# Token norms taken on columns of tokens, and the recurrent layer's norm moved between the two halves of its first head's contraction

## The chip, the core and the metric

The kernel runs on one core of one Trainium2 chip. The metric is the device time of one execution in microseconds, as a median over runs. The engines named below are PE (TensorE), DVE (VectorE), ACT (ScalarE), POOL (GpSimd) and SP (SyncE, which issues all transfers here); each runs its own instructions in order and they wait for each other through semaphores.

## The reference, cut to what matters

Two residual layers over 2048 tokens of 1024 features, each behind an RMS norm, and a last norm:

```python
def rms_norm(x, w):
    y = x * lax.rsqrt(jnp.mean(x * x, axis=-1, keepdims=True) + RMS_EPS)
    return y * w
...
h = rms_norm(x, norm_w[0]);  x = x + chunked_sgu_mixer(h, ...)   # widths 3 * 2048, then back
h = rms_norm(x, norm_w[1]);  x = x + rglru_mixer(h, ...)         # 12 heads of 128, gate path, scan
return rms_norm(x, norm_f_w)
```

The mean is over the 1024 features of one token, so a norm is one number for each token.

## The kernel before

Features lie on the 128 partitions and tokens along the free axis, so a tile is 128 features by 512 tokens. The tokens are worked in two blocks of 1024 (`i` = 0, 1), each in two halves of 512 (`th`). A product in full precision is made of three matmuls on rounded parts (`mm3`, L286): each operand is split by ACT into a rounded copy (L80) and by DVE into what is left of it (L81).

For each block the program runs: the first norm (`Half.norm`, names `a`), the value projection (`pv`), the gated products (`J`, `Y`, `ps`), the output products (`X`, `Y`, `Z`), the second norm (names `b`), the recurrent layer's heads (`px`, `pg`, then `pr` and `pi` for its gates), its output products (`po`), and the last norm (names `f`). The program's `f` norms of block 0 are written into block 1's value projection, and block 1's `a` norms into block 0's last `po` products.

A norm works like this. `Norm.add` squares each tile on ACT and adds it to an accumulator `sa` of 128 by 512 on DVE. `Norm.finish` multiplies `sa` by a 128 by 128 matrix of ones (`st`, L400), so that all 128 partitions hold the sum of each of the 512 tokens, and takes the root in `rsqrt` on the whole 128 by 512: `nm` on ACT (L374), the square root on ACT (L375), then on DVE a reciprocal (L376) and one step of refinement (L377 to L379). Its result `r` (called `ra`, `rbb`, `rf`) then scales the tiles.

In the recurrent layer the norm is applied behind the projection, since the scale of a token commutes with it: `Head.conv` multiplies the finished `px` by `rb` (L718), convolves (L725, L729), splits the result into `xch` (L734) and `xcl` (L735), and `gates` multiplies these by the gate weights into `pr` and `pi`. The first head (`n` = 0) contracts its 1024 features in two halves `u`, in the order `px` half 0, `pg` half 0, `px` half 1, `pg` half 1; `after(0, 0)` then calls `finish_b`, the two halves of the norm. Head 1's `px` and head 0's `gates` follow.

A scheduler places the instructions of each engine by readiness and priority, so the written order is only a preference. Accumulators of three tiles of two banks (`pj`) and two of one bank (`pb`) are shared by everything on PE; split weights go round in eight buffers (`wops`), and their raw loads in four (`raws`).

Of the kernel before, what the change touches and what calls it, by code (L numbers as in the profile page):

```python
# [9 lines left out]
F32 = mybir.dt.float32  # L10
F32R = mybir.dt.float32r
AF = mybir.ActivationFunctionType
ALU = mybir.AluOpType

P = 128
D = 1024
# [5 lines left out]
TB = 2 * T  # L22
# [29 lines left out]
def trunk(ctx: ExitStack, tc: tile.TileContext, xT, WI, WV, WB, WO, WG, par, wsT, bs, outT):  # L52
    nc = tc.nc

    const = ctx.enter_context(tc.tile_pool(name="const", bufs=1))
# [4 lines left out]
    work = ctx.enter_context(tc.tile_pool(name="work", bufs=12))  # L60
# [3 lines left out]
    def pj(name):  # L64
        return pjp.tile([P, 2, T], F32, tag="pj", name=name)

    def pb(name):
        return pbp.tile([P, T], F32, tag="pb", name=name)

    def wk(name):  # L70
        return work.tile([P, 1032], F32, tag="wk", name=name)[:, :TB].rearrange(
            "p (a t) -> p a t", a=2
        )

    def sm(name, tag="sm"):
        return smp.tile([P, T], F32, tag=tag, name=name)
# [136 lines left out]
    for i in range(NB):  # L213
# [10 lines left out]
        if i == 0:  # L224
            for k in (0, 4):
                n = ahead.pop(0)
# [43 lines left out]
    def take(key):  # L270
        def load(key, make, load):
            if load is not None:
                load()

        def make(key, make, load):
            t = make()
            if key is not None:
                ready[key] = t

        advance(loads, at[key] + FAR, load)  # L280
        advance(makes, at[key] + LOOK, make)
        return ready.pop(key)

    def mm3(out, sh, sl, mh, ml, first, last):
        for n, (s, m) in enumerate(((sh, mh), (sh, ml), (sl, mh))):
            nc.tensor.matmul(  # L286
                out, lhsT=s, rhs=m, start=first and n == 0, stop=last and n == 2,
                skip_group_check=True,
            )
# [5 lines left out]
    def col(c):  # L295
        return pp[:, c : c + 1]

    ones = const.tile([P, P], F32, name="ones")
    eps = const.tile([P, 2], F32, name="eps")
    halo = const.tile([P, NH, 3], F32, name="halo")  # L300
    state = const.tile([P, NH], F32, name="state")
    c8 = const.tile([P, NH], F32, name="c8")
# [4 lines left out]
        nc.tensor.matmul(warm[:, :P], lhsT=ones, rhs=ones, start=True, stop=True)  # L307
    nc.gpsimd.memset(eps[:, 0:1], RMS_EPS)
    nc.gpsimd.memset(eps[:, 1:2], LN_EPS)
    nc.gpsimd.memset(halo, 0.0)  # L310
    nc.gpsimd.memset(state, 0.0)

# [59 lines left out]
    def rsqrt(r, x, m, t, scale, e):  # L372

        nc.scalar.activation(m, x, AF.Identity, bias=eps[:, e : e + 1], scale=scale)  # L374
        nc.scalar.activation(r, m, AF.Sqrt)  # L375
        nc.vector.reciprocal(r, r)  # L376
        nc.vector.tensor_tensor(t, r, r, ALU.mult)  # L377
        nc.vector.scalar_tensor_tensor(t, t, -0.5, m, ALU.mult, ALU.mult)
        nc.vector.scalar_tensor_tensor(r, t, 1.5, r, ALU.add, ALU.mult)  # L379

    class Norm:
# [5 lines left out]
        def add(self, t, eng=nc.vector):  # L387
            for kk in range(2):
# [6 lines left out]
                    eng.tensor_tensor(self.acc, self.acc, q, ALU.add)  # L395
                self.n += 1

        def finish(self, r):
            st = pb(f"st_{self.name}")
            nc.tensor.matmul(st, lhsT=ones, rhs=self.acc, start=True, stop=True)  # L400
            rsqrt(r, st, sm(f"nm_{self.name}"), self.acc, 1.0 / D, 0)

    xv = xT.rearrange("(g k a p) t -> g a p k t", g=2, k=2, a=2, p=P)
    ov = outT.rearrange("(g k a p) t -> g a p k t", g=2, k=2, a=2, p=P)
# [50 lines left out]
    class Pair:  # L455


        def __init__(self, i, m, tp, outs, c21, finish):
            self.i, self.m, self.tp, self.outs = i, m, tp, outs
            self.c21, self.finish = c21, finish  # L460
            self.id = f"{i}_{m}"
# [101 lines left out]
    def y_tile(name):  # L563
        return tc.dram_tile([2, 2, P, 2, T], F32, name=name)
# [139 lines left out]
    class Head:  # L704
# [9 lines left out]
        def conv(self, px, rb):  # L714

            n = self.n
            xb = work.tile([P, 1032], F32, tag="wk", name=f"xb{self.id}")
            nc.vector.tensor_tensor(  # L718
                xb[:, 3 : 3 + TB].rearrange("p (a t) -> p a t", a=2), px, rb, ALU.mult
            )  # L720
            nc.gpsimd.tensor_copy(xb[:, 0:3], halo[:, n, :])
            nc.gpsimd.tensor_copy(halo[:, n, :], xb[:, TB : TB + 3])
            xc = self.xc = wk(f"xc{self.id}")
            xf = self.flat(xc)
            nc.scalar.activation(  # L725
                xf, xb[:, 3 : 3 + TB], AF.Identity, bias=col(C_CB + n), scale=col(C_CW + 4 * n + 3)
            )
            for k in range(3):
                nc.vector.scalar_tensor_tensor(  # L729
                    xf, xb[:, k : k + TB], col(C_CW + 4 * n + k), xf, ALU.mult, ALU.add  # L730
                )
            self.ch = work.tile([P, 2, T], F32R, tag="wk", name=f"xch{self.id}")
            self.cl = work.tile([P, 2, T], F32R, tag="wk", name=f"xcl{self.id}")
            nc.scalar.copy(self.ch, xc)  # L734
            nc.vector.tensor_tensor(self.cl, xc, self.ch.bitcast(F32), ALU.subtract)  # L735
# [44 lines left out]
    def b_branch(i, hb, rb, hooks):  # L780

        yd = [y_tile(f"yb{i}_{r}") for r in range(3)]
        gw = {}
        heads = [Head(i, n, gw, yd) for n in range(NH)]

        def proj(out, n, z, us=(0, 1)):
            for u in us:
                w = take((i, "b", n, z, u))
                for a, th in ((0, 0), (1, 1), (0, 1), (1, 0)):
                    t = hb[a, th, u]  # L790
                    for kk in range(2):
                        o = (2 * kk + a) * P
                        mm3(
                            out[:, th], w[:, 0, o : o + P], w[:, 1, o : o + P], t[:, 0, kk],
                            t[:, 1, kk], u == 0 and a == th and kk == 0,
                            u == 1 and a != th and kk == 1,
                        )

        def after(n, k):
            for f in hooks.get((n, k), ()):  # L800
                f()

        for n in range(NH):
            px = pj(f"px{i}_{n}")
            if n == 0:
                pg = pj(f"pg{i}_{n}")
                for u in range(2):
                    proj(px, n, 0, (u,))
                    proj(pg, n, 1, (u,))
                after(0, 0)  # L810
            else:
                proj(px, n, 0)
                heads[n - 1].gates()
            heads[n].conv(px, rb)
            if n > 0:
                heads[n - 1].decay()
                pg = pj(f"pg{i}_{n}")
                proj(pg, n, 1)
            heads[n].silu(pg, rb)
            if n > 0:  # L820
                heads[n - 1].scan()
            after(n, 1)
        return yd, heads[-1]
# [105 lines left out]
    for i in range(NB):  # L929
# [40 lines left out]
        def ready_b(g, a, th, i=i, x=x, xd=xd, nm=nm, hb=hb):  # L970

            def f():
                t = x[a, th, g]
                nc.sync.dma_start(xd[a, th, g], t)
                o = hb[a, th, g] = top(f"hb{i}_{a}{th}{g}")
                for kk in range(2):
                    w = col(C_NB + 4 * g + 2 * kk + a)
                    nc.scalar.activation(o[:, 0, kk], t[:, kk], AF.Copy, scale=w)
                    nc.vector.scalar_tensor_tensor(
                        o[:, 1, kk], t[:, kk], w, o[:, 0, kk].bitcast(F32), ALU.mult, ALU.subtract  # L980
                    )
                nm[th].add(t)
            return f

        after = {
            (g, p): [ready_b(g, a, th)]
            for g in range(2)
            for p, a, th in ((2, 0, 0), (7, 1, 1), (3, 0, 1), (4, 1, 0))
        }
# [13 lines left out]
        def get_y(r, i=i, y=y):  # L1003
            def f():
                y[r] = load_yb(i, r, yd)
            return f

        yd, tail = b_branch(i, hb, rb, {(0, 0): [finish_b]})
        y[0] = load_yb(i, 0, yd)
        x = {}  # L1010
# [124 lines left out]
```

## Time and profile before

| | |
|---|---|
| median of 3 runs | 2289.09 us (2287.63 to 2290.79) |
| the profiled execution, its own time | 2292.71 us |
| its span in the profile | 2291.0 us |
| PE busy / DVE busy / ACT busy | 97% / 69% / 46% of the span |
| mean granted clock of PE | 0.99 |
| transfers | 327.84 MB, 41% of 16 engines' span |

The span runs from the first to the last instruction that the profile records; the execution's own time is 1.7 us longer, and 3.6 us above the median of the runs. PE's busy share counts matmuls from start to modelled end, so an interval in which PE has waited shows as an entry of the waits, and one in which it was slow as a granted clock below 1.

### The profile page before, as it was taken

To read this page: it belongs to the slowest core of one execution; us is meant where nothing else is said; L and a number is where in the kernel's file an instruction comes from. 1 tells how busy PE (TensorE), PEld (TensorE's weight loads), DVE (VectorE), ACT (ScalarE), POOL (GpSimd) and SP (SyncE) were. 2 spreads that over 40 slices of the span, in tenths; PEclk is the share of its full clock that TensorE was granted. 3 is DMA by queue.
4 is the path that set the end of the run, shared out by engine and by line. 5 is a ranking of instruction groups with operands and counts; after the bars stand their busy time and mean duration, and the time that the engine had idled before them with its cause. 6 is when DMAs were issued, how large, how long until landed. Compare 5 with 4: busy or idle time off the path is not lost.

```text
span 2291.0 us, 25466 instructions
## 1 busy us (share of the span) xinstructions
PE 2213.1 (97%) x9872; PEld 1821.4 (80%) x9872; DVE 1575.7 (69%) x1936; ACT 1057.3 (46%) x1377; POOL 63.2 (3%) x82
## 2 busy tenths in 40 slices
PE   5999999999999899999999999999999989999996
PEld 4787888888788688888788888888878868888884
DVE  6957787676777677775693266676669766776736
ACT  4434444443215677774342144444412347767611
POOL 0000000000000001000000000000000000110000
PEclk9999999999999999999999999999999989999998
DMA  4788353327764122226143233322487512321411
GB/s 148 262 310 307 127 180 111 110 83 270 276 231 141 51 88 88 95 102 231 37 166 110 74 110 111 102 94 100 162 311 256 194 60 69 106 92 65 176 45 74
DMA packets 124040, 327.84 MB, mean 143 GB/s; under 512 B 9616, under 2 KB 26128, under 8 KB 123920
## 3 DMA queue, kind: packets, MB, share of 16 engines
q1 hardware_dynamic: 123920, 326.22, 41.0%
q8 instruction: 77, 1.26, 0.2%
q14 instruction: 43, 0.35, 0.0%
HBM read 232.34 MB, written 93.85 MB: 142 GB/s over the span
## 4 chain that ended last, share of the span: by engine, by line
PE 85%; DVE 8%; DMA 3%; issue 2%; ACT 1%; SPq 0%; DVEq 0%; ACTq 0%
PE J L286 20%; PE pv L286 13%; PE pg L286 11%; PE px L286 10%; PE po L286 10%; PE X L286 6%; PE Y L286 5%; PE Z L286 3%; PE ps L653 2%; PE pr L286 2%; PE pi L286 2%; DMA keep<-wc 1%; DVE ya L81 1%; DMA x<-in_xT 1%; DVE xr L873 0%
## 5 line engine op out<-in xcount | busy, mean ns | idle before, releaser
L286 PE MATMUL pv<-wv,b 128*128 128x512 f32 x1536 | 357.9, 395 | 19.6 <-ACT b L80 15.8
L286 PE MATMUL J<-ha,w 128*128 128x512 f32 x1536 | 368.9, 391 | 0.5 <-DVE u_2b L494 0.5
L286 PEld LDWEIGHTS pv<-wv,b 128*128 128x128 f32 x1536 | 291.4, 190 | 86.4 <-ACT b L80 17.8
L286 PEld LDWEIGHTS J<-ha,w 128*128 128x128 f32 x1536 | 287.6, 188 | 61.5 <-DVE u_2b L494 0.9
L286 PE MATMUL po<-yb,wo 128*128 128x512 f32 x1152 | 265.6, 392 | 2.6 <-DVE xr L862 2.6
L286 PE MATMUL pg<-hb,wb 128*128 128x512 f32 x1152 | 266.6, 390 | 0.0
L286 PE MATMUL px<-hb,wb 128*128 128x512 f32 x1152 | 266.6, 390 | 0.0
L286 PEld LDWEIGHTS po<-yb,wo 128*128 128x128 f32 x1152 | 217.3, 189 | 49.7 <-DVE xr L862 3.0
L286 PEld LDWEIGHTS pg<-hb,wb 128*128 128x128 f32 x1152 | 217.1, 188 | 46.0
L286 PEld LDWEIGHTS px<-hb,wb 128*128 128x128 f32 x1152 | 216.3, 188 | 45.8 <-PE st_b L400 0.5
L286 PE MATMUL J<-b,w 128*128 128x512 f32 x768 | 186.8, 391 | 0.3 <-DVE w L81 0.3
L286 PE MATMUL X<-ya,w 128*128 128x512 f32 x768 | 184.1, 390 | 2.3 <-ACT ya L80 1.3
L286 PEld LDWEIGHTS X<-ya,w 128*128 128x128 f32 x768 | 143.6, 188 | 34.0 <-DVE x L550 2.2
L286 PEld LDWEIGHTS J<-b,w 128*128 128x128 f32 x768 | 142.9, 188 | 30.0 <-DVE w L81 0.7
L80 ACT CAST w<-raw 128x512 fp32r<-128x512 f32 x160 | 99.3, 622 | 139.7 <-issue 66.9
L81 DVE TENSOR_TENSOR w<-raw,w 128x512 fp32r<-128x512 f32 x160 | 109.7, 688 | 61.6 <-ACT w L80 61.2
L80 ACT CAST ya<-ya 128x1024 fp32r<-128x1024 f32 x56 | 57.0, 1049 | 170.7 <-DVE ya L449 92.7
L80 ACT CAST wb<-rb 128x512 fp32r<-128x512 f32 x96 | 58.8, 616 | 99.9 <-PE px L286 49.2
L550 DVE TENSOR_TENSOR x<-x,X 128x1024 f32<-128x1024 f32 x64 | 78.0, 1218 | 35.2 <-PE X L286 35.1
L286 PE MATMUL Z<-ya,w 128*128 128x512 f32 x384 | 94.3, 391 | 3.1 <-DVE ya L81 2.7
L729 DVE SCALAR_TENSOR_TENSOR xc<-xb,pp,xc 128x1024 f32<-128x1024 f32 x72 | 92.3, 1282 | 4.3 <-ACT xc L725 3.5
L286 PE MATMUL Y<-b,w 128*128 128x512 f32 x384 | 93.5, 392 | 0.8 <-DVE sp L657 0.6
(344 smaller groups left out, 2868.0 us busy)
## 6 DMA issues: line engine op xcount, KB each, us to landing
w<-keep SPq DMA_DIRECT2D x112, 512.0 KB, 3.8
raw<-in_w SPq DMA_DIRECT2D x64, 512.0 KB, 3.5
keep<-wc SPq DMA_DIRECT2D x56, 512.0 KB, 5.7
rb<-in_wb SPq DMA_DIRECT2D x48, 512.0 KB, 3.4
rv<-in_v SPq DMA_DIRECT2D x32, 512.0 KB, 4.3
vd<-v SPq DMA_DIRECT2D x32, 512.0 KB, 4.4
vl<-vd SPq DMA_DIRECT2D x32, 512.0 KB, 4.7
ya<-ya SPq DMA_DIRECT2D x16, 1024.0 KB, 5.8
```

The costliest lines, as they stand in the source:

```text
L80: nc.scalar.copy(dst[:, 0], src)
L81: nc.vector.tensor_tensor(dst[:, 1], src, dst[:, 0].bitcast(F32), ALU.subtract)
L286: nc.tensor.matmul(out, lhsT=s, rhs=m, start=first and n == 0, stop=last and n == 2, skip_group_check=True,)
L550: nc.vector.tensor_tensor(t, t, acc[z], ALU.add)
L653: nc.tensor.matmul(pS[:, n * P : (n + 1) * P], lhsT=v[j][th][:, n, cc * P : (cc + 1) * P], rhs=wcv[:, j, :], start=True, stop=True,)
L729: nc.vector.scalar_tensor_tensor(xf, xb[:, k : k + TB], col(C_CW + 4 * n + k), xf, ALU.mult, ALU.add)
```

## The change

The sum over features is now taken with the roles turned: 128 tokens of `sa` are the weights and one column of ones is streamed (`columns`), so `st` holds a token's sum on its own partition, 128 tokens in each of 4 columns. The root is taken by the same six instructions on 128 by 4 elements, in place, in the first columns of `sa`. `row` brings it back onto all partitions: DVE multiplies an identity matrix by each column (128 by 128, four times), PE multiplies ones by that diagonal into `bc`, and ACT copies the 128 by 512 result to `r`. POOL makes the identity once at the start. In the first head of the recurrent layer, `after(0, 0)` is called behind the first half `u` = 0 instead of behind both. Two lines shrink a buffer and a descriptor area to make room for the identity.

```diff
@@ const
+    ident = const.tile([P, P], F32, name="ident")
...
+    nc.gpsimd.affine_select(
+        out=ident, in_=ones, pattern=[[1, P]], compare_op=ALU.is_equal, fill=0.0, base=0,
+        channel_multiplier=-1,
+    )
@@ class Norm
+        def columns(self):
+            st = pb(f"st_{self.name}")
+            for n in range(4):
+                nc.tensor.matmul(
+                    st[:, n : n + 1], lhsT=self.acc[:, n * P : (n + 1) * P], rhs=ones[:, 0:1],
+                    start=True, stop=True,
+                )
+            c = self.c = self.acc[:, 0:12].rearrange("p (k n) -> p k n", k=3)
+            rsqrt(c[:, 0], st[:, 0:4], c[:, 1], c[:, 2], 1.0 / D, 0)
+            return c[:, 0]
+
+        def row(self, r):
+            d = sm(f"nd_{self.name}")
+            b = pb(f"bc_{self.name}")
+            for n in range(4):
+                ns = slice(n * P, (n + 1) * P)
+                nc.vector.tensor_scalar(d[:, ns], ident, self.c[:, 0, n : n + 1], None, ALU.mult)
+                nc.tensor.matmul(b[:, ns], lhsT=ones, rhs=d[:, ns], start=True, stop=True)
+            nc.scalar.copy(r, b)
+
         def finish(self, r):
-            st = pb(f"st_{self.name}")
-            nc.tensor.matmul(st, lhsT=ones, rhs=self.acc, start=True, stop=True)
-            rsqrt(r, st, sm(f"nm_{self.name}"), self.acc, 1.0 / D, 0)
+            self.columns()
+            self.row(r)
@@ b_branch
                 for u in range(2):
                     proj(px, n, 0, (u,))
                     proj(pg, n, 1, (u,))
-                after(0, 0)
+                    if u == 0:
+                        after(0, 0)
@@ wk, conv
-        work.tile([P, 1032], F32, tag="wk", ...)
+        work.tile([P, 1028], F32, tag="wk", ...)
@@ kernel
-    nc = bacc.Bacc("TRN2", target_bir_lowering=False, num_devices=1, dynamic_dma_scratch_size=1024)
+    nc = bacc.Bacc("TRN2", target_bir_lowering=False, num_devices=1, dynamic_dma_scratch_size=512)
```

**PE at the recurrent layer's first head, block 0.** `pg_0`, `px_0` and `px_1` are the accumulators of heads 0 and 1; the suffix `_0` or `_1` of `st_b` and `bc_b` is the half of the tokens. Before:

```order
L286 MATMUL pg_0_5200<-hb_100_5016,wb_01_0_5107 128x512 x6
L286 MATMUL px_0_5199<-hb_001_5096,wb_00_1_5137 128x512 x6
L286 MATMUL px_0_5199<-hb_111_5124,wb_00_1_5137 128x512 x6
L286 MATMUL px_0_5199<-hb_011_5154,wb_00_1_5137 128x512 x6
L286 MATMUL px_0_5199<-hb_101_5184,wb_00_1_5137 128x512 x6
...
L286 MATMUL pg_0_5200<-hb_101_5184,wb_01_1_5167 128x512 x6
L400 MATMUL st_b_0_5313<-sa_b_0_4940,ones 128x512
L400 MATMUL st_b_1_5322<-sa_b_1_4966,ones 128x512
L286 MATMUL px_1_5347<-hb_000_4935,wb_10_0_5201 128x512 x6
```

After the change, at the same place on PE (the line numbers are those of the changed file):

```order
L286 MATMUL pg_0_5228<-hb_100_5044,wb_01_0_5135 128x512 x6
L407 MATMUL st_b_0_5285<-ones,sa_b_0_4968 128x1 x4
L286 MATMUL px_0_5227<-hb_001_5124,wb_00_1_5165 128x512 x6
L286 MATMUL px_0_5227<-hb_111_5152,wb_00_1_5165 128x512 x6
L286 MATMUL px_0_5227<-hb_011_5182,wb_00_1_5165 128x512 x3
L422 MATMUL bc_b_0_5297<-nd_b_0_5296,ones 128x128 x4
L407 MATMUL st_b_1_5307<-ones,sa_b_1_4994 128x1 x4
L286 MATMUL px_0_5227<-hb_011_5182,wb_00_1_5165 128x512 x3
L286 MATMUL px_0_5227<-hb_101_5212,wb_00_1_5165 128x512 x6
L422 MATMUL bc_b_1_5319<-nd_b_1_5318,ones 128x128 x4
L286 MATMUL pg_0_5228<-hb_001_5124,wb_01_1_5195 128x512 x6
```

The sums of the first half of the tokens moved ahead of 48 products (`px_0` and `pg_0`, second half), and the broadcasts stand between them, 15 products behind the first sums and 9 behind the second.

**ACT at the same place.** `wb` is a split weight, `xc` the convolution, `xch` its rounded copy. Before, and then after:

```order
L80 CAST wb_20_0_5377<-rb_20_5228 128x512
L80 CAST wb_20_1_5404<-rb_20_5228 128x512
L80 CAST wb_21_0_5449<-rb_21_5284 128x512
L374 ACTIVATE nm_b_0_5315<-st_b_0_5313,eps 128x512
L375 ACT_TABLE_LOAD
L375 ACTIVATE rbb_5195<-nm_b_0_5315 128x512
L374 ACTIVATE nm_b_1_5324<-st_b_1_5322,eps 128x512
L375 ACTIVATE rbb_5195<-nm_b_1_5324 128x512
```

```order
L80 CAST wb_20_0_5431<-rb_20_5256 128x512
L379 ACTIVATE sa_b_0_4968<-st_b_0_5285,eps 128x4
L380 ACT_TABLE_LOAD
L380 ACTIVATE sa_b_0_4968<-sa_b_0_4968 128x4
L423 COPY rbb_5223<-bc_b_0_5297 128x512
L379 ACTIVATE sa_b_1_4994<-st_b_1_5307,eps 128x4
L380 ACTIVATE sa_b_1_4994<-sa_b_1_4994 128x4
L80 CAST wb_20_1_5458<-rb_20_5256 128x512
L423 COPY rbb_5223<-bc_b_1_5319 128x512
L751 ACTIVATE xc_0_5389<-xb_0_5385,pp 128x1024
L80 CAST wb_21_0_5503<-rb_21_5356 128x512
L760 CAST xch_0_5394<-xc_0_5389 128x1024
```

Two casts of weights that stood ahead of the roots now stand behind the first root, one of them ahead of the second copy.

**DVE at the last norm of block 0, inside block 1's value projection.** `xa`, `xt` and `ha` belong to block 1's gated products, `nd_f` is the diagonal. Before, and then after:

```order
L81 TENSOR_TENSOR b_011_8168<-xt_1_7612,b_011_8168 128x1024
L81 TENSOR_TENSOR b_111_8171<-xt_1_7612,b_111_8171 128x1024
L376 RECIPROCAL rf_0_8186<-rf_0_8186 128x512
L376 RECIPROCAL rf_1_8232<-rf_1_8232 128x512
L377 TENSOR_TENSOR sa_f_0_7857<-rf_0_8186 128x512
L377 TENSOR_TENSOR sa_f_1_7862<-rf_1_8232 128x512
```

```order
L381 RECIPROCAL sa_f_0_7937<-sa_f_0_7937 128x4
L475 TENSOR_TENSOR xa_001_7659<-xt_1_7666,xa_001_7659 128x1024
L382 TENSOR_TENSOR sa_f_0_7937<-sa_f_0_7937 128x4
L81 TENSOR_TENSOR ha_0_5_8433<-xa_000_7655,ha_0_5_8433 128x1024
L383 SCALAR_TENSOR_TENSOR sa_f_0_7937<-sa_f_0_7937 128x4
L475 TENSOR_TENSOR xt_0_7663<-xt_0_7663 128x1024
L384 SCALAR_TENSOR_TENSOR sa_f_0_7937<-sa_f_0_7937 128x4
L475 TENSOR_TENSOR xa_000_7655<-xt_0_7663,xa_000_7655 128x1024
L421 TENSOR_SCALAR nd_f_0_8278<-ident,sa_f_0_7937 128x128 x4
```

Four tiles of 128 by 1024 now stand between the steps of that root, and PE's broadcast of it comes 30 products behind its sums.

## Rows read from the trace of the kernel before

**Rows 1.** The page's chain that ended last, shares of the span by engine.

```profile
PE 85%; DVE 8%; DMA 3%; issue 2%; ACT 1%; SPq 0%; DVEq 0%; ACTq 0%
```

**Rows 2.** Waits of PE: releaser, us in total, times, longest.

```profile
PE pr L286 <- ACT xch L734: 18.4, 2, 9.2
```

**Rows 3.** Timeline, second norm of block 0: start, us, what [idle before <-releaser].

```profile
722.58 0.62 ACT L80 CAST wb<-rb 128x512 fp32r<-128x512 f32 x1 [2.54 <-PE pg L286]
...
733.26 1.88 PE L400 MATMUL st_b<-sa_b,ones 128*128 128x512 f32 x4
...
734.58 11.49 PE L286 MATMUL px<-hb,wb 128*128 128x512 f32 x48
...
735.03 1.28 ACT L375 ACT_TABLE_LOAD   x1
736.32 0.63 ACT L375 ACTIVATE rbb<-nm_b 128x512 f32<-128x512 f32 x1
...
736.99 6.57 DVE L376 RECIPROCAL rbb<-rbb 128x512 f32<-128x512 f32 x2 [2.18 <-ACT rbb L375]
...
747.62 1.22 DVE L718 TENSOR_TENSOR xb<-px,rbb 128x1024 f32<-128x1024 f32 x1
...
755.28 0.80 PE L286 MATMUL pr<-xch,wg 128*128 128x512 f32 x1 [9.21 <-ACT xch L734]
...
760.98 11.37 PE L286 MATMUL pg<-hb,wb 128*128 128x512 f32 x48
```

**Rows 4.** Busy by stretch: us, PE, PEld, DVE, ACT, POOL, granted clock, DMA share, GB/s.

```profile
757.00:759.00 2.00, 2.00 (x6) 1.52 (x6) 1.76 (x2) 1.32 (x2) 0.11 (x1) 0.50 0.00 0
```

**Rows 5.** The chain in order of time: start, us, what.

```profile
772.35 10.88 PE px L286 x48
```

**Rows 6.** Instructions of the root's lines and L640: ns min/median/max, first and last start.

```profile
L374 ACT ACTIVATE rstd<-mv,eps x2: 301/302/302, 222.7 to 1338.3; 128x8 f32<-128x8 f32 x2
...
L376 DVE RECIPROCAL rbb<-rbb x4: 3294/3324/3353, 737.0 to 1856.1; 128x512 f32<-128x512 f32 x4
...
L376 DVE RECIPROCAL rstd<-rstd x2: 195/199/203, 224.9 to 1340.1; 128x8 f32<-128x8 f32 x2
...
L640 DVE TENSOR_SCALAR vl<-vl,mv,rstd x128: 404/409/416, 226.1 to 1627.0; 128x256 f32<-128x256 f32 x128
```

**Rows 7.** Timeline of PE where full-precision matmuls of 128 columns run.

```profile
254.34 1.95 PE L653 MATMUL ps<-wcT,vl 128*128 128x128 f32 x16
256.04 2.32 PE L286 MATMUL J<-b,w 128*128 128x512 f32 x9
```

**Rows 8.** Timelines of the start, PE and DVE.

```profile
12.85 2.08 PE L400 MATMUL st_a<-sa_a,ones 128*128 128x512 f32 x2 [7.16 <-DVE sa_a L395]
...
25.61 5.39 DVE L910 SCALAR_TENSOR_TENSOR xa<-xa,pp,ra 128x512 f32<-128x512 f32 x8
...
47.50 9.45 PE L286 MATMUL pv<-wv,b 128*128 128x512 f32 x39
...
59.51 1.20 PE L286 MATMUL pv<-wv,b 128*128 128x512 f32 x4 [2.57 <-ACT b L80]
61.70 20.02 PE L286 MATMUL pv<-wv,b 128*128 128x512 f32 x80 [0.99 <-DVE b L81]
```

**Rows 9.** Busy by stretch, two later stretches, columns as in rows 4.

```profile
125.00:225.00 100.00, 98.84 (x434) 80.86 (x432) 65.83 (x107) 46.25 (x72) 0.00 (x0) 1.00 0.86 310
...
1157.00:1190.00 33.00, 33.00 (x144) 26.56 (x142) 32.58 (x40) 10.06 (x14) 0.00 (x0) 1.00 0.45 153
```

**Rows 10.** Timeline of PE in block 0's last output products.

```profile
1139.52 18.21 PE L286 MATMUL po<-yb,wo 128*128 128x512 f32 x72 [2.60 <-DVE xr L862]
```

**Rows 11.** Timeline of the end, PE and DVE.

```profile
2251.46 16.93 PE L286 MATMUL po<-yb,wo 128*128 128x512 f32 x72
...
2273.05 1.50 PE L400 MATMUL st_f<-sa_f,ones 128*128 128x512 f32 x2 [4.66 <-DVE sa_f L395]
...
2281.60 5.39 DVE L873 SCALAR_TENSOR_TENSOR xr<-xr,pp,rf 128x512 f32<-128x512 f32 x8
```

More of the change, by code (lines that the diff above doesn't have):

```diff
@@ L70, in wk @@
     def wk(name):
-        return work.tile([P, 1032], F32, tag="wk", name=name)[:, :TB].rearrange(
+        return work.tile([P, 1028], F32, tag="wk", name=name)[:, :TB].rearrange(
             "p (a t) -> p a t", a=2
@@ L716, in conv @@
             n = self.n
-            xb = work.tile([P, 1032], F32, tag="wk", name=f"xb{self.id}")
+            xb = work.tile([P, 1028], F32, tag="wk", name=f"xb{self.id}")
             nc.vector.tensor_tensor(
```

## The prediction

> **What bounds the kernel now.** I read the page's chain first: it lies on PE for 85% of the span [rows 1], so a change pays only where PE stands still or runs slowly, or where it adds work to PE. Next the waits of PE: the largest is not weights but `pr` waiting for `xch`, 18.4 us in two waits of 9.2 [rows 2]. The timeline of one of them shows why [rows 3]. The sums of the norm start at 733.26, behind both halves of head 0's contraction. The roots, with two reciprocals of 128 by 512 in 6.57 us, let `xb` start only at 747.62, and `xch` releases `pr` at 755.28. PE has by then finished the 48 products of `px_1` and waited 9.21 us. The 12 gate products that follow run at the lower clock level (0.50 granted, 1.2 GHz [rows 4]) after that idle time: from 755.28 to 760.98 is 5.70 us, where 48 products take 10.88 us at full clock [rows 5] and 12 would take 2.72. So one site loses 9.2 + 3.0 = 12.2 us, and there are two, one per block. The other waits of PE that a norm causes are smaller: at the start and behind the first half [rows 8], in block 0's last `po` [rows 10], and at the end, where nothing else is left to run [rows 11].
>
> **The change part by part.** *Prices.* A root on 128 by 4 is nearest to the `rstd` one on 128 by 8: 0.30 us for the first ACT pass and 0.2 for a reciprocal, which takes 3.32 on 128 by 512 [rows 6]; I take 0.2 for each of the other four short steps. A diagonal piece (128 by 128, one scalar) is not in the trace; between the short ops' 0.2 and `L640`'s 0.409 on 256 columns [rows 6] I take 0.3, so four cost 1.2, from 0.8 to 1.6. Full-precision matmuls appear as two instructions each. Sixteen of 128 columns occupy PE from 254.34 to 256.04 [rows 7], 0.106 each, so a broadcast of four matmuls costs 0.85. The old sum streams the same number of columns, so it cancels. What is new on PE is the columns: eight instructions that each load a full 128 by 128 weight but stream one column. Their cost lies between nothing and 0.85; I take 0.85, since the weight loads are those of [rows 7]. The copy back I take as 0.6, like the root in [rows 3]. One finish thus costs PE 0.85 more and takes some 5 us less of DVE.
>
> The shorter chain from sums to `r` is, at full clock, 0.85 (columns) + 0.3 + 0.2 + 0.8 (four short DVE steps) + 1.2 + about 0.3 (last broadcast piece) + 0.6 = 4.25 us.
>
> *The recurrent layer's norm, twice.* At 722.4 `pg`'s first half ends: the cast at 722.58 is released by it [rows 3]. In the new order of PE the columns run to 723.25. The pass, a table load of 1.28 [rows 3], root, four short steps and four products give 727.05. PE has 15 products (3.4 us) as cover, to 726.65, so it waits 0.4. The second half's chain needs no load: 2.5 us over nine products of 2.04, a wait of 0.5. ACT also holds a cast between that root and the copy. It waits for `px_0`'s second half, which PE has finished before that broadcast, so it delays little. `r` is complete at about 731.8. From `xb` to the release of `pr` the trace has 755.28 - 747.62 = 7.7 us [rows 3], which gives 739.5. PE meanwhile does 96 products (21.76), two columns, two broadcasts (3.4) and waits 0.9, and reaches `pr` at 748.5. So `xch` is early by 9 us: the wait is gone, the clock stays up, and `pg_1` starts near 751.2 instead of 760.98. **-9.8 us, twice: -19.6.** What is late next is nothing on PE; the cover can shrink by 9 us before the wait returns.
>
> *The start.* The chain from 12.85 to the scaling at 25.61 [rows 8] becomes 1.7 (columns, 0.85 doubled, since the old sum took 2.08 there, at the lower clock) + 0.3 + 1.28 (load) + 0.2 + 0.8 + 1.2 and six splits of weights on DVE that the order keeps between these steps (0.67 each, as a scaling pass in [rows 8]): 22.4. **-3.1.** Behind the first half PE ends its 39 products near 57.0, then waits 2.57 and 0.99, and 80 products take 20.02 instead of 18.1 [rows 8]: 5.5 us. The second half's norm is 3.1 to 4 us shorter and its casts are ordered ahead of the eviction that delayed them. Less 0.85 and 0.9 of waits at the broadcast: **-3.7.**
>
> *Block 1's first norms, inside `po`.* The wait of 2.60 comes because DVE evicts late, and 72 products then take 18.21 instead of 16.3 [rows 10]; with some 10 us less of DVE work both go (4.3 with the 0.2 by which the modelled end of such a run lies late). PE pays two columns and about 0.9 of waits: **-1.7.**
>
> *Block 0's last norms, inside `pv`.* Here PE waits for nothing before, while DVE is busy 32.58 of 33 us [rows 9]. The new order puts four tiles of about 1.2 us between the steps of the first root. Pass, root, steps, tiles and products make 7.4 us against 30 products (6.8) of cover on PE; the second root is interleaved in the same way. Two columns and about 2 us of waits: **+3.7.** If there were no cover at all, it would be 7 us more for each.
>
> *The end.* The chain from 2273.05 to the last scaling at 2281.60 is 8.55 us [rows 11]. It becomes 1.7 (columns, at the lower clock) + 0.3 + 0.2 + 0.8 + 1.2 + 0.4 + 0.6 = 5.2. The earlier half's scaling leaves DVE free when `po` ends near 2268.2, about 0.5 us earlier in spite of 0.85 more on PE. **-3.7.**
>
> *The rest.* The identity is one POOL op before the first transfer has landed, the two sizes move no instruction: 0.
>
> Sum: -19.6 - 3.1 - 3.7 - 1.7 + 3.7 - 3.7 = -28.1 us on the profiled span of 2291.0, whose own time is 2292.7, 3.6 us above the median of the runs. I apply it to the median: 2289.1 - 28.1 = **2261.0 us**.
>
> **The rivals.** *The early gain is swallowed by transfers.* From 125 to 225 us the transfer engines are busy 0.86 of the time at 310 GB/s while PE still runs 98.84 of 100 us [rows 9]. If the weights there can't come earlier, the 6.8 us of the start are given back: 2267.8. For it: the high share. Against: those transfers are issued as buffers come free, which moves with PE.
>
> *A smaller bill on PE.* If a one-column matmul costs next to nothing and the broadcasts are never waited for, the ten finishes inside PE's stream save 0.85 each, and 5 us of waits go as well: 2248 at the least, about 2254 if half of that holds. The full weight loads speak against.
>
> *A hold behind the table load.* In rows 3 the root starts 1.29 us after the table load does, so the load costs its 1.28 and no more. If ACT were held once more as long behind it, the new chains would be late at their first broadcast in both blocks and at the start, by 1.3 each: 2265. The trace speaks against it. The Trainium skill, "ScalarE: Activation LUTs", section "What ACT_TABLE_LOAD costs", states such a hold: a drain of about 1.38 us behind each load, 2.66 in all; by that the sum would be 4 us smaller.
>
> *The broadcasts become the wait (the other side).* PE runs in order, so each `bc` holds all products behind it until DVE has written the diagonals. At ten places in PE's stream (one in block 0's start, four `b`, two `a`, two `f`, the first `f` of block 1) a queue on DVE or ACT is then paid on PE, and a long one costs the clock too, as in rows 4. At 1 us more at each the time is 2271; it turns slower than before from 2.8 us more at each, where the whole 28.1 are gone. For it: DVE's full stretch [rows 9]. Against: at the two largest places DVE and ACT wait for PE and are not full.
>
> *The wait only moves.* If `r` came 9 us later than worked out, `pr` would wait as before and the gain would be the small sites alone, about 8 us: 2281. Nothing in the order stands between to make it so late.
>
> **How the numbers follow.** The forecast (2256 to 2266) has 0.55, transfers swallowing the start 0.15, the smaller bill 0.12, broadcasts waiting 0.5 to 2 us more each 0.08, the table load 0.02, the wait that moves 0.02, slower 0.03, no change 0.03. The range reaches from the smaller bill to the broadcasts at 1 us each: 2252 to 2272. A measurement of this kernel tells 0.2% (4.6 us) from no change; all cases but the last two are faster by more: 0.94, 0.03, 0.03.
>
> **What would show it.** In the changed profile: no wait of `pr` for `xch`, and 12 gate products at full clock; `xb` of head 0 before `px_1` ends; no idle of PE between the halves of the first `pv`; `bc` waits for DVE of under 1 us each and the longest at the `f` of block 0; the last scaling some 5 us behind the last sums. The prediction is wrong if the waits at `bc` add up to more than 10 us, or if the span shortens at the start but the stretch from 125 to 225 us grows by as much.

## The result and the profile after

| | before | after |
|---|---|---|
| median, first comparison | 2288.36 us (2287.39 to 2290.79) | 2257.84 us (2256.75 to 2258.75) |
| median, a second comparison on one chip | 2290.96 us (2286.45 to 2292.91) | 2257.28 us (2256.21 to 2257.78) |
| ratio, first and second | | 0.9865 [0.9848, 0.9882], 0.9855 [0.9838, 0.9871] |
| profiled execution, own time and span | 2292.71, 2291.0 us | 2257.38, 2255.7 us |

The change makes the kernel 30.5 us faster in the first comparison and 33.7 us in the second; 2261.0 was forecast. The two profiled executions stand 35.3 us apart, since the one of before lies 4.4 us above its median and the one of after 0.5 below.

The page's chain by engine in the changed kernel, which answers to [rows 1]:

```profile
PE 94%; DVE 3%; DMA 1%; ACT 1%; issue 0%; SPq 0%; DVEq 0%; ACTq 0%
```

Its waits of PE, which answer to [rows 2]:

```profile
PE st_a L407 <- DVE sa_a L400: 6.7, 1, 6.7
PE bc_a L422 <- DVE nd_a L421: 5.0, 1, 5.0
PE st_f L407 <- DVE sa_f L400: 3.6, 1, 3.6
PE pv L286 <- ACT b L80: 3.2, 1, 3.2
...
PE bc_f L422 <- DVE nd_f L421: 1.8, 1, 1.8
```

PE holds 94% of the chain where it held 85%. The wait of `pr` is gone from the list, and of the twelve broadcasts only the first and the last are waited for, at the two ends of the program where PE has nothing else to do. The timeline around the second norm of block 0, which answers to [rows 3] (all times 8.0 us earlier from the start's gain):

```profile
714.40 0.94 PE L407 MATMUL st_b<-ones,sa_b 128*128 128x1 f32 x8
715.21 3.71 PE L286 MATMUL px<-hb,wb 128*128 128x512 f32 x15
715.39 0.26 ACT L379 ACTIVATE sa_b<-st_b,eps 128x4 f32<-128x4 f32 x1 [0.17 <-PE st_b L407]
715.67 1.28 ACT L380 ACT_TABLE_LOAD   x1
716.96 0.21 ACT L380 ACTIVATE sa_b<-sa_b 128x4 f32<-128x4 f32 x1
...
718.01 0.87 DVE L421 TENSOR_SCALAR nd_b<-ident,sa_b 128x128 f32<-128x128 f32 x4
718.76 1.05 PE L422 MATMUL bc_b<-nd_b,ones 128*128 128x128 f32 x8
719.65 0.95 PE L407 MATMUL st_b<-ones,sa_b 128*128 128x1 f32 x8
...
723.73 0.59 ACT L423 COPY rbb<-bc_b 128x512 f32<-128x512 f32 x1 [0.27 <-PE bc_b L422]
724.35 1.22 DVE L744 TENSOR_TENSOR xb<-px,rbb 128x1024 f32<-128x1024 f32 x1 [0.17 <-ACT rbb L423]
...
730.94 1.05 ACT L760 CAST xch<-xc 128x1024 fp32r<-128x1024 f32 x1 [1.11 <-DVE xc L755]
...
739.89 0.40 PE L286 MATMUL pr<-xch,wg 128*128 128x512 f32 x1
...
742.68 1.55 PE L286 MATMUL pg<-hb,wb 128*128 128x512 f32 x6
```

`xch` is complete at 731.99 and PE reaches `pr` at 739.89 without waiting: 7.9 us to spare. The 12 gate products take 2.79 us, and the stretch's granted clock is 1.00 (columns as in [rows 4]):

```profile
739.90:742.70 2.80, 2.80 (x14) 2.26 (x13) 1.83 (x2) 2.58 (x3) 0.00 (x1) 1.00 0.00 0
```

Where the 35.3 us come from is read from the first and last start of PE's products of one accumulator in one block. For the kernel before (`px` of block 0; `pv`, `px` and `po` of block 1):

```profile
L286 PE MATMUL px<-hb,wb x576: 387/389/793, 708.8 to 1004.0; 128*128 128x512 f32 x192
L286 PE MATMUL pv<-wv,b x768: 387/389/799, 1157.6 to 1333.5; 128*128 128x512 f32 x192
L286 PE MATMUL px<-hb,wb x576: 387/389/793, 1824.6 to 2120.0; 128*128 128x512 f32 x192
L286 PE MATMUL po<-yb,wo x576: 387/389/799, 2133.9 to 2268.0; 128*128 128x512 f32 x192
```

and for the changed one:

```profile
L286 PE MATMUL px<-hb,wb x576: 387/389/486, 700.8 to 985.4; 128*128 128x512 f32 x192
L286 PE MATMUL pv<-wv,b x768: 387/389/486, 1136.4 to 1313.9; 128*128 128x512 f32 x192
L286 PE MATMUL px<-hb,wb x576: 387/389/486, 1802.8 to 2087.3; 128*128 128x512 f32 x192
L286 PE MATMUL po<-yb,wo x576: 387/389/486, 2101.2 to 2236.2; 128*128 128x512 f32 x192
```

Differences of these starts, with block 0's first `po` (1017.9 before, 999.3 after) and the spans, give the gain of each stretch:

| stretch | gained, us | forecast |
|---|---|---|
| start to first `px` | 8.0 | 6.8 |
| recurrent layer, block 0 | 10.6 | 9.8 |
| `po` with block 1's first norms | 2.6 | 1.7 |
| `pv` with block 0's last norms | -1.6 | -3.7 |
| block 1 from there to `px` (not changed) | 2.2 | 0 |
| recurrent layer, block 1 | 10.9 | 9.8 |
| last `po` and the end | 2.6 | 3.7 |
| sum | 35.3 | 28.1 |

The largest maximum in these rows, 793 and 799 ns before and 486 after, is no sign of the clock. The one `px` product of 793 ns in block 0 starts at 734.6, directly behind the old sums over 512 columns, at a granted clock of 1.00. With full-width sums it is back in a kernel whose PE waits for nothing there (the wide roots for the recurrent layer alone, below):

```profile
L286 PE MATMUL px<-hb,wb x576: 387/389/793, 701.3 to 984.0; 128*128 128x512 f32 x192
```

### The profile page after: what moved, and what is told of

Read it like the earlier page. It is cut to its first block, busy times and chain, and to the rows that moved or that the text cites. A ratio compares the mean times of both kernels' runs of the same rounds, so it can differ in the third digit from the quotient of the medians.

```text
span 2255.7 us, 25881 instructions
## 1 busy us (share of the span) xinstructions
PE 2214.7 (98%) x10040; PEld 1836.0 (81%) x10040; DVE 1533.0 (68%) x1984; ACT 1054.7 (47%) x1389; POOL 64.3 (3%) x83
## 3 DMA queue, kind: packets, MB, share of 16 engines
q8 instruction: 79, 1.29, 0.2%
## 4 chain that ended last, share of the span: by engine, by line
PE 94%; DVE 3%; DMA 1%; ACT 1%; issue 0%; SPq 0%; DVEq 0%; ACTq 0%
PE J L286 22%; PE pv L286 15%; PE px L286 12%; PE pg L286 12%; PE po L286 12%; PE X L286 7%; PE Y L286 5%; PE Z L286 4%; PE ps L679 2%; PE pi L286 1%; PE pr L286 1%; DVE ya L81 1%; DMA raw<-in_w 1%; DVE ya L475 0%; DMA ya<-ya 0%
## 5 line engine op out<-in xcount | busy, mean ns | idle before, releaser
L286 PEld LDWEIGHTS X<-ya,w 128*128 128x128 f32 x768 | 143.6, 188 | 32.7 <-ACT ya L80 2.1
```

The costliest lines, as they stand in the source:

```text
L286: nc.tensor.matmul(out, lhsT=s, rhs=m, start=first and n == 0, stop=last and n == 2, skip_group_check=True,)
```

## The experiments

Each was timed against the kernel before on its own chip (medians 2290.91, 2290.96 and 2289.25 us there); "less" below is against that. All of them keep the identity and the two smaller sizes.

**Columns without the move.** The call stands behind both halves again.

```diff
-                    if u == 0:
-                        after(0, 0)
+                after(0, 0)
```

> All norms on columns, but the recurrent layer's norm is called behind both halves of the first head, as before the change. Theory (the place gives most of the recurrent layer's gain, since it puts 48 more products of head 0 over the chain): from the end of pg's second half, columns, root and both broadcasts make r ready about 9.5 us later and xch about 7.7 us behind that, 17.2 in all, while px_1's 48 products, the columns and the broadcasts cover 14.3; pr waits about 2.9 us per block and the gate products run slowly again, so some 5 us of the 10.3 to 10.9 stay per block: time 2270 (2266 to 2276). Rival (the shorter root alone takes the wait away, the place is free): no wait of pr, 2256 to 2260.

Measured: 2268.44 us, 22.5 less, ratio 0.9903 [0.9889, 0.9917]. The wait of `pr`, first in the waits of PE, then in PE's timeline of block 0:

```profile
PE pr L286 <- ACT xch L760: 5.7, 2, 2.9
```

```profile
743.08 0.79 PE L286 MATMUL pr<-xch,wg 128*128 128x512 f32 x1 [2.87 <-ACT xch L760]
```

The wait is the 2.9 us worked out. The recurrent layer gains 4.8 and 6.0 us per block (first `px` to first `po`, as in the table) in place of 10.6 and 10.9. The blocks differ behind the wait: the 12 gate products take 5.3 us in block 0 and 4.7 in block 1, where the clock rose sooner. The rival falls: the shorter root alone doesn't hide the chain.

**The move without columns.** `finish` is the old one for all norms; the call stays between the halves.

```diff
         def finish(self, r):
-            self.columns()
-            self.row(r)
+            st = pb(f"st_{self.name}")
+            nc.tensor.matmul(st, lhsT=ones, rhs=self.acc, start=True, stop=True)
+            rsqrt(r, st, sm(f"nm_{self.name}"), self.acc, 1.0 / D, 0)
```

> All roots on the full 128 by 512 as before the change; only the recurrent layer's norm is put between the halves of the first head. Theory (place): from the sums, xch was released 22.0 us later in the profile of before, and PE now has 1.3 us of sums and 96 products (21.8 us) over it, 23.1 us; pr waits at most 1 to 2 us, and about 12 us are gained per block, more than with columns, since no columns and no broadcasts stand on PE: 2264 to 2267. Rival (the shorter root is needed for it): a wait of pr of 4 us or more stays with its slow gate products, 2274 or more.

Measured: 2263.85 us, 27.1 less, 0.9883 [0.9869, 0.9896]. In block 0:

```profile
720.87 1.88 PE L431 MATMUL st_b<-sa_b,ones 128*128 128x512 f32 x4
...
742.26 1.05 ACT L765 CAST xch<-xc 128x1024 fp32r<-128x1024 f32 x1 [2.49 <-DVE xc L760]
...
744.39 0.40 PE L286 MATMUL pr<-xch,wg 128*128 128x512 f32 x1
```

`xch` is complete at 743.31, 1.1 us before PE asks for it, and no wait is left (1 to 2 us were thought possible). The recurrent layer gains 12.6 and 12.7 us, more than with columns. The place alone takes the wait away; the columns give it some 7 us more slack, which nothing uses, and cost PE 2 us per block.

**Wide roots for the recurrent layer alone.** For this and the next ones `finish` chooses between both versions by the norm's name.

```diff
         def finish(self, r):
-            self.columns()
-            self.row(r)
+            if not self.name.startswith("b"):
+                self.columns()
+                self.row(r)
+            else:
+                st = pb(f"st_{self.name}")
+                nc.tensor.matmul(st, lhsT=ones, rhs=self.acc, start=True, stop=True)
+                rsqrt(r, st, sm(f"nm_{self.name}"), self.acc, 1.0 / D, 0)
```

> The changed kernel with the full-width root for the recurrent layer's norm alone (still between the halves); the other norms stay on columns. Theory (place): per block 2 columns (0.81) and 2 broadcasts (0.87) leave PE and 1.3 us of sums come back, so 2 us less per block if the wait of pr stays away: 2253 to 2255. Rival (the columns are needed there): the wait comes back, 2268 or more.

Measured: 2254.01 us, 36.9 less, 0.984 [0.9827, 0.9854]. No wait of `pr`; the recurrent layer gains 12.5 and 12.6.

**The column matmuls twice.**

```diff
+            for n in range(4):
+                nc.tensor.matmul(
+                    st[:, 4 + n : 5 + n], lhsT=self.acc[:, n * P : (n + 1) * P], rhs=ones[:, 0:1],
+                    start=True, stop=True,
+                )
```

> The changed kernel with the column matmuls of every norm issued a second time into unused columns of st, which changes no result. Theory (a column matmul costs its full weight load, eight instructions in 0.81 us at full clock and 1.87 at the lower one): ten sets stand in PE's stream at full clock and two at the start and the end at the lower one, 8.1 + 3.7 = 11.8 us: 2268 to 2270. Rival (one column costs next to nothing, the 0.81 is the change of weights around it): 2258 to 2260.

Measured: 2272.49 us, 18.4 less, 15.2 above the changed kernel's second median (of another comparison). PE, block 0:

```profile
716.76 0.95 PE L407 MATMUL st_b<-ones,sa_b 128*128 128x1 f32 x8
717.57 1.03 PE L412 MATMUL st_b<-ones,sa_b 128*128 128x1 f32 x8
718.47 3.71 PE L286 MATMUL px<-hb,wb 128*128 128x512 f32 x15
```

A set takes 0.81 to 0.90 us from start to start, and in the profiles each stretch of the table with two sets at full clock loses 1.7 to 1.9 us against the changed kernel, and the start 2.8. So one streamed column costs PE nearly what 128 do, and the rival falls. The sum was 3.4 us short of the medians, and the time lies outside the range: 1.8 us are lost in block 1 between `pv` and `px`, where no set stands; PE waits there for DVE for 1.3 us that the changed kernel's profiles don't have. Of the other 1.6, some 0.5 lie in the sets, since the second of a pair takes 0.90 and not 0.81, and 1.1 outside the span, which ends 2.8 us short of the execution's own time here (2269.7 of 2272.49) and 1.7 in the changed kernel. Why it does is open.

**Columns and move for the recurrent layer alone** (`startswith("b")` takes the columns). The changed kernel ran beside this one and the next two; for it was written:

> The changed kernel once more, as the companion of the next three on one chip; from its first comparison it stands 30.5 us below the kernel before (29 to 33 here).

> Columns and the move for the recurrent layer's norm alone; the norms of the first layer and the last norms on the full 128 by 512 as before. Theory (the parts add up): 10.6 to 10.9 us per block remain and the start, the norms in po and pv and the end fall away: 21 to 22.5 us below the kernel before, against about 9 us that these others give. Rival (the parts share a gain, for instance through when weights arrive): more than 25 us below.

Measured: 2257.28 us for the changed kernel and 2269.50 for this one, 33.7 and 21.5 less (0.9911 [0.9897, 0.9926]). The parts add up: 10.6 and 10.8 us per block here, and 12.2 for all the other norms together (about 9 were expected), of which block 1's first ones have their wait back in this kernel:

```profile
PE po L286 <- DVE xr L894: 2.6, 1, 2.6
```

The clock did not fall behind that wait here: the 72 products take 16.6 us, where they took 18.2 before and in the move without columns behind the same 2.6.

**Wide roots for block 0's last norms alone** (`not startswith("f0")` takes the columns).

> The changed kernel with the full-width root for block 0's last norms alone, those inside block 1's value projection. Theory (there the columns only add two sets of column matmuls to PE, 1.6 us, and hide no wait): 1.6 us faster than the changed kernel, between 1 and 2.5, and the broadcasts' place shows no wait. Rival (the 5 us of DVE that the columns save there per norm are needed by block 1's first tiles): slower than the changed kernel by 1 us or more, with a wait of PE on DVE between 1140 and 1200 us.

Measured: 2257.15 us, 0.13 below the changed kernel: the whole time can't tell. The stretch can. `pv` of block 1 in this kernel, then in the changed one of the same chip:

```profile
L286 PE MATMUL pv<-wv,b x768: 387/389/799, 1136.6 to 1312.3; 128*128 128x512 f32 x192
```

```profile
L286 PE MATMUL pv<-wv,b x768: 387/389/486, 1136.0 to 1313.6; 128*128 128x512 f32 x192
```

175.7 against 177.6 us: 1.9 us less, and PE waits for nothing there. In the profiled pair, 0.6 of it had been lost ahead of that stretch and 0.8 is given back behind it, where the two programs are the same.

**Wide roots for both of these** (columns for `a` and for block 1's `f`).

> Full-width roots for the recurrent layer's norm, moved between the halves, and for block 0's last norms; columns for the first layer's norms and the final ones. Theory (columns pay only where PE waits for the root or DVE is late): 2 us per block and 1.6 us less than the changed kernel, 5.6 us in all: 35 to 38 us below the kernel before. Rival (DVE becomes late somewhere with four full-width roots per block back): no better than the changed kernel.

Measured: 2251.69 us, 39.3 less, 0.9831 [0.9816, 0.9846], and 5.6 below the changed kernel on the same chip, as summed. The 39.3 lie above the 35 to 38 named, since the changed kernel itself is 33.7 below here and not 30.5. This version beats both kernels.

**A longer root.** The refinement is repeated three times in `columns`.

```diff
             rsqrt(c[:, 0], st[:, 0:4], c[:, 1], c[:, 2], 1.0 / D, 0)
+            for _ in range(3):
+                nc.vector.tensor_tensor(c[:, 2], c[:, 0], c[:, 0], ALU.mult)
+                nc.vector.scalar_tensor_tensor(c[:, 2], c[:, 2], -0.5, c[:, 1], ALU.mult, ALU.mult)
+                nc.vector.scalar_tensor_tensor(c[:, 0], c[:, 2], 1.5, c[:, 0], ALU.add, ALU.mult)
```

> The changed kernel with the refinement step of every root done four times instead of once: nine more short DVE steps of 0.2 us per norm, 1.8 us more between columns and broadcast. The scheduler answers by putting bc_b 22 and 20 products behind the columns instead of 15 and 9. Theory (the place of a broadcast in PE's order follows the chain, so PE does not wait for it; the recurrent layer has some 8 us of slack before pr): no wait of bc in the recurrent layer, none of pr, and the time grows only where nothing covers the chain, 1.8 us at the start and 1.8 at the end: 3 to 6 us above the changed kernel. Rival (each broadcast holds PE for what the chain grows by): 1.8 us at ten places and at the end, 18 us or more above it.

Measured: 2262.45 us, 26.8 less; its profiled span is 2261.1 us, 5.8 above that of the changed kernel's second profile. Waits of PE, and PE in block 0:

```profile
PE bc_a L426 <- DVE nd_a L425: 8.5, 2, 8.3
...
PE bc_f L426 <- DVE nd_f L425: 3.6, 1, 3.6
```

```profile
718.00 5.29 PE L286 MATMUL px<-hb,wb 128*128 128x512 f32 x22
723.14 1.05 PE L426 MATMUL bc_b<-nd_b,ones 128*128 128x128 f32 x8
...
725.38 4.28 PE L286 MATMUL pg<-hb,wb 128*128 128x512 f32 x18
729.85 1.13 PE L426 MATMUL bc_b<-nd_b,ones 128*128 128x128 f32 x8 [0.19 <-DVE nd_b L425]
```

The chain grows by 1.8 us and PE waits 0.19 for one broadcast of the block, none for `pr`: 22 and 20 products now stand ahead of the broadcasts. Nearly all is paid at the ends, 3.3 us more at the first `bc_a` (weight splits stand between the added steps too) and 1.8 at the last `bc_f`. The rival of waits at ten places falls.

**Also the first half of block 1's last norms wide.**

> The kernel with wide roots for the recurrent layer's and for block 0's last norms, and now also for the first half of block 1's last norms, inside the last output products. Theory (PE pays 1 us less, but the wide root and the scaling behind it keep DVE from the last two sums, which were 1.3 us later behind the products before the change): no difference to the kernel without it beyond 1 us. Rival (only the PE bill counts): 1 us faster, 38 to 41 us below the kernel before.

Measured: 2252.06 us, 37.2 less, 0.9836 [0.9822, 0.9849]; against 2251.69 (39.3 less, on another chip) no gain, and the intervals overlap. What PE saves goes into the last sums, 3.6 us behind the products in the changed kernel and here as late as before [rows 11]:

```profile
PE st_f L431 <- DVE sa_f L400: 4.7, 1, 4.7
```

## Why the prediction was right

Over the changed stretches of the profiled pair the terms add to 28.1 us where 33.1 were gained, and the medians of the first comparison show 30.5. Five stretches came out better than forecast, by 6.1 us together, and the end 1.1 worse.

**The recurrent layer (9.8 forecast, 10.6 and 10.9).** The mechanism holds step by step: less the 8.0 us of the start, `r` was due at 723.8 and was complete at 724.3, `xch` at 731.5 (731.99), `pr` at 740.5 (739.89). The term was small by the 0.9 us of waits at the broadcasts, which did not come; against them, PE takes 25.5 us from the columns to `pr` (714.40 to 739.89) where the sum without these waits has 25.2. The step "PE has 15 products as cover, so it waits 0.4" held the first broadcast until all four diagonals were done; it follows the first, and the four take 0.87, not 1.2. Some 0.3 us more come from `pg_1`, whose 48 products no longer begin at a low clock (11.07 against 11.37 in [rows 3], where the granted clock is 0.93 from 761 to 765). The argument left one thing out: the sum credited the gain to the short chain and the move together. Measured apart, the move alone gives 12.6 us, the columns alone 4.8, both together 10.6 (block 0). The slack of 9 us that I counted was the sign: the old chain, longer by about 7, would have fitted too.

**The start (6.8, 8.0).** In the changed kernel, PE and DVE:

```profile
12.42 1.87 PE L407 MATMUL st_a<-ones,sa_a 128*128 128x1 f32 x8 [6.72 <-DVE sa_a L400]
...
21.98 5.39 DVE L937 SCALAR_TENSOR_TENSOR xa<-xa,pp,ra 128x512 f32<-128x512 f32 x8 [0.46 <-ACT ra L423]
...
55.07 11.24 PE L286 MATMUL pv<-wv,b 128*128 128x512 f32 x48 [0.17 <-DVE b L81]
```

The first scaling begins at 21.98, 3.6 us earlier (3.1 forecast), of which 0.4 lie ahead of the sums (12.42 in place of 12.85). The chain from there takes 9.6 us and the terms add to 9.5, but that is luck: the sum left out the end of the broadcast and the copy (2.2 us from the last diagonal at 19.73), and it counted six splits of weights between the steps where three stand (the steps with the splits take 2.7 us in place of 4.8). Behind the first scaling 5.5 us more are gained by the last `pv` product (9.1 us earlier) in place of 3.7: the idle time between the halves is 0.17 us, the 0.9 of waits at the broadcast did not come, and 0.9 of waits of `pv` for `v` went too, which I had not counted. The transfers did not swallow it: first `rs` is 7.7 us earlier. Until `px` 1.1 us are given back, where the changed kernel's profile waits 1.7 us at `Y` for `sp` and the one of before doesn't. The size is uncertain by about 1 us: two kernels with the old start (move alone; recurrent layer alone) reach `px` at 707.3 and 709.1, against 708.8.

**Block 1's first norms (1.7, 2.6).** The wait of `po` and its slow products are gone, and the 0.9 us of waits at the broadcasts did not come.

**Block 0's last norms (-3.7, -1.6).** The two columns cost what was summed, 1.7 (0.81 each in the trace); the 2 us of waits were wrong. In the changed kernel, PE and DVE there:

```profile
1141.80 0.95 PE L407 MATMUL st_f<-ones,sa_f 128*128 128x1 f32 x8
...
1142.61 7.11 PE L286 MATMUL pv<-wv,b 128*128 128x512 f32 x30
...
1148.15 0.86 DVE L421 TENSOR_SCALAR nd_f<-ident,sa_f 128x128 f32<-128x128 f32 x4
...
1149.56 1.05 PE L422 MATMUL bc_f<-nd_f,ones 128*128 128x128 f32 x8
```

The diagonals end at 1149.01, 6.4 us behind the columns (1142.61), where I had 7.4: the four short steps and the four tiles take 4.8 us (1143.32 to 1148.15) in place of 5.6, and the diagonals 0.86 in place of 1.2. The 30 products cover 6.9 us, so PE comes 0.55 us after the last diagonal. Ahead of the second broadcast stand 51 products, and PE comes 0.7 us after its diagonals.

**The end (3.7, 2.6).** PE's wait ahead of the last sums is 3.56 us in place of 4.66 [rows 11], a gain of 1.1, while the first half's columns and broadcast cost PE 0.9 (the last `po` product starts 31.8 us earlier, the first one 32.7). The chain behind the sums was mis-sized: from 8.55 to 6.37 us, not to 5.2.

```profile
2240.14 1.86 PE L407 MATMUL st_f<-ones,sa_f 128*128 128x1 f32 x8 [3.56 <-DVE sa_f L400]
...
2243.81 2.04 PE L422 MATMUL bc_f<-nd_f,ones 128*128 128x128 f32 x8 [1.80 <-DVE nd_f L421]
...
2246.51 5.39 DVE L900 SCALAR_TENSOR_TENSOR xr<-xr,pp,rf 128x512 f32<-128x512 f32 x8 [2.26 <-ACT rf L423]
```

I gave the lower clock to the columns and not to the broadcast: PE has waited 3.56 and 1.80 us, its granted clock in both stretches is 0.50, the lower level of 1.2 GHz, and the eight instructions take 2.04 us and end 1.6 behind the last diagonal, where I had 0.4. The row of the first stretch (columns as in [rows 4]):

```profile
2240.10:2242.00 1.90, 1.86 (x8) 1.78 (x8) 0.00 (x0) 0.00 (x0) 0.00 (x0) 0.50 0.00 0
```

**The rest (0, 2.2).** The profiled execution of before waits 1.6 us in block 1's products between `pv` and `px` (0.6 at `Y` for `sp`, 1.0 at `X` for `x`), the changed one doesn't. The move alone shows 1.7 us in the same stretch, the recurrent layer alone 1.6, and the columns without the move 2.1. So this gain takes neither the columns nor the move. No run separates that one execution of before from the identity and the two smaller sizes, which all later kernels share. Waits of this sort do come and go for one kernel: at block 0's `Y` the two profiles of the changed kernel wait 1.7 and 1.0 us for `sp`. They may be part of why the profiled pair differs by more than the medians.

**The rivals.** Transfers, the smaller bill on PE, the wait that only moves and the waits at broadcasts are answered above. The table load: its root starts 1.29 us after the load does in the changed kernel too (715.67, 716.96), so no hold stands behind it, and the pass ahead of it ends at 715.65, so none stands there either. The Trainium skill, "ScalarE: Activation LUTs", section "What ACT_TABLE_LOAD costs", adds a drain of about 1.38 us to the load's 1.28, 2.66 in all, which I had read as behind the load; here the measurement decides. For the bill on PE the Trainium skill, "TensorE: Matmul & The Clock Gate", section "LDWEIGHTS (loading the stationary operand)", lets the columns of the weight alone set the time of its load, 128 / 1.2 = 107 ns; eight loads would be 0.85 us, an estimate, and the trace agrees with 0.81 to 0.90 for a set. Of what I said the profile would show, three things were wrong: no broadcast at block 0's `f` waits, those at the two ends wait 5.0 and 1.8 us and not under 1, and the last scaling comes 6.4 us behind the last sums, not 5.

## What to carry to other kernels

Before shortening a small chain that a full engine waits for, look whether an earlier place in the order hides it as it is: here the place alone gave 12.6 us per block and the shorter chain took 2 of them back. A rewrite that moves work onto the engine that bounds the kernel pays only where that engine stands and waits or the relieved engine is late (here the start, block 1's first norms and the end), so choose it norm by norm: the mixed version is 5.6 us faster than the uniform one. A broadcast in an in-order queue cost a wait of 0.2 us at most here where its place followed the length of the chain.

## What the runs showed of the hardware

- A full-precision matmul that streams one column occupies PE nearly as long as one of 128: eight instructions in 0.81 us (714.40 to 715.21) beside 0.89 (718.76 to 719.65).
- A granted clock of 1.00 recorded at a program's start does not show that PE ran at it. Eight column instructions take 1.87 us there, as at the end (1.86), yet the changed kernel's profile has 1.00 for the first stretch (12.40 to 14.30) and 0.50 for the second. Between 12.0 and 14.6, five of the twelve profiles record 1.00 and seven 0.50, and the instructions take as long in both: 1.87 us again in the kernel with wide roots for block 0's last norms, at 0.50. So the pace is that of the lower level, as the prediction took it to be.
- The clock does not fall behind every wait of one length: after 2.60 us without a product in `po`, the mean granted clock of the next stretch was 0.91 before (1139 to 1158) and 1.00 in the kernel with columns for the recurrent layer alone (1127 to 1146).
- A full-precision sum of two instructions of 512 columns delays the next product too. In the kernel with wide roots for block 0's last norms, 24 `pv` products with such a sum behind them take 5.44 us (1136.61 to 1142.05); with the sum itself 0.46 us to the next start, and the next 24 products then take 5.90 (1142.51 to 1148.41). So the sum costs some 0.9 us, as much as the four broadcast matmuls.
- Four short DVE steps that depend on each other start 0.2 us apart (717.20, 717.42, 717.61, 717.81) and last 0.16 to 0.18; four independent diagonal pieces of 0.28 us each end 0.87 us after the first starts.
